# Zero products and reordered loads in the first stage, and another pacing of the gate sums and dots, in a two-layer diffusion backbone

## Chip, core and metric

One core of a Trainium2 chip runs the whole kernel in one launch. The metric is device microseconds of one execution. The kernel before took 2444.27 us (median of 3 runs, 2444.13 to 2444.34).

## What is computed

Two layers over 256 latent tokens (2048 wide, float32) and 256 context tokens. Each sub-layer is modulated by six vectors (shift, scale and gate for the mixer, and the same for the FFN) that come from a matrix product of SiLU(c) with `ada_w`.

```python
for i in range(DEPTH):                                  # 2 layers
    sh1, sc1, g1, sh2, sc2, g2 = split(silu(c) @ ada_w[i] + ada_b[i], 6)
    a = h * (1 + sc1) + sh1
    if i == 0:                                          # neighbourhood attention, context keys included
        csh1, csc1, ... = split(silu(c_ctx) @ ada_w[0] + ada_b[0], 6)
        ac = ctx * (1 + csc1) + csh1
        y = attention(a @ w_qkv, ac @ w_kv) @ w_o       # 16 heads of 128
    else:                                               # gMLP on chunks of 128 positions
        u, v = split(gelu(a @ w_in)); y = (u * (W_s @ ln(v) + b)) @ w_out
    h = layer_norm(ALPHA * h + g1 * y)
    h = layer_norm(ALPHA * h + g2 * swiglu(h * (1 + sc2) + sh2))   # FFN, inner width 5632
```

## The kernel before

Precision. Every large matrix product is done with three TensorE products: both operands are split into a rounded high part and a low part (`split_into`: ScalarE casts, VectorE subtracts), and high x high, high x low and low x high are summed in PSUM (`mm3`, lines 89 to 91). So every weight piece of 128 x 1024 costs ScalarE a cast, VectorE a subtraction whose two inputs lie in SBUF, and TensorE its products. `prefetch` keeps up to `pos["bufs"] - 1` pieces split ahead: two in the attention, four later.

First stage. Shift and scale of the mixer of layer 0 are needed for all 16 blocks (kt) of 128 columns before anything else. Block kt's scale is a TensorE dot (`dot`): 16 small float32 products with `c_pad` (SiLU(c) and SiLU(c_ctx), padded to 32 columns) in four column groups, then a copy to a row (ScalarE) and small products that gather the groups (`gather`, line 363). The shift is done so for kt < DVE0 = 3. From DVE0 on it is a VectorE dot (`dot_dve`): two passes over a 128 x 2048 tile of the transposed matrix, one for each condition. `modulate` then makes the block's activations on ScalarE and splits them. In the loop over kt TensorE does the keys of three heads, the dots of a block ahead (kt + 2 from kt = 2 on), the values of four token blocks, and from kt = 3 on an early piece of other keys. Loads go out from SP's queue in program order: `ap` (1 MB each, two a block, in four slots), `xt`, `rkv`. Small loads (`badj`, `ident`, `sel`) go out from ScalarE's queue, the rows of c and c_ctx from SP's, and GpSimd broadcasts them.

Tasks. The other modulation vectors are made in the background. A list of tasks stands in a fixed order: dots (VectorE, 1.2 us each, line 153) and gate products (VectorE multiplies and adds a 128 x 1024 piece into `gate`, line 177). After the 32 products of one gate vector a sum task runs an all-reduce over partitions on GpSimd (line 192). Each task costs 0.5 credits. Every step of the main loops calls `tick(n)`, which adds n x rate credits and runs the tasks that they pay for; `pace(units)` sets the rate to all open credits over a number of units. A tick that has a side task (an affine step or a transposition of the FFN) counts 0.3. In the attention a piece of keys or values counts 2 units and half a query projection 1, 124 in all. An FFN has 172 ticks in its gate and up blocks (two blocks of 512 columns in turn, eight weight pieces each, the first with four), and its down-projection 78 more. `need(...)` runs what is left of a vector where it is used. Gate products and dots are pinned in VectorE's order; otherwise a scheduler orders each engine's instructions by priority. GpSimd has only sums, broadcasts of rows and memsets.

Accumulators. Four PSUM tiles (`acc`) serve the gate and the up product of a block in turn; the down-projection needs all four at once, so it waits until VectorE has multiplied `sg` (line 820).

Of the kernel before, what the change touches and what calls it, by code (L numbers as in the profile page):

```python
# [11 lines left out]
F32 = mybir.dt.float32  # L12
F32R = mybir.dt.float32r
BF16 = mybir.dt.bfloat16
AF = mybir.ActivationFunctionType
ALU = mybir.AluOpType
# [3 lines left out]
P = 128  # L20
D = 2048
NT = 256
KT = D // P
# [12 lines left out]
MASKED = -1e30  # L36

SH1, SC1, G1, SH2, SC2, G2 = range(6)
HK0 = 3
RAW = 4  # L40
ADA = 6
FETCH = 5
SCRATCH = 4096
BUSY = 0.3
DVE0 = 3
W0 = HK0 * P + 512
EARLY = tuple((3 + 4 * g + h, h, 4 * g) for g in range(3) for h in range(4))
EN = 4
EARLY_END = {HK0 + h: 12 for h in range(4)}


@with_exitstack
def hybrid_kernel(ctx: ExitStack, tc: tile.TileContext, i, out):
    nc = tc.nc
    V, S, T = nc.vector, nc.scalar, nc.tensor
# [1 line left out]
    outer = ctx.enter_context(tc.tile_pool(name="outer", bufs=1))  # L57

    c_col = outer.tile([P, KT, 2], F32, tag="ccol", name="c_col")
    nc.sync.dma_start(c_col, i["c_col"])  # L60
    badj = outer.tile([P, 2, 6, KT], F32, tag="badj", name="badj")
    nc.scalar.dma_start(badj, i["ada_b_col"])
    ident = outer.tile([P, P], F32, tag="ident", name="ident")
    nc.scalar.dma_start(ident, i["ident"])
    eps_t = outer.tile([P, 1], F32, tag="eps", name="eps_t")
    nc.gpsimd.memset(eps_t, EPS)
    warm = outer.tile([P, 1], F32, tag="warm", name="warm")
    S.activation(c_col, c_col, AF.Silu)
    for t in (SC1, SC2):
        V.tensor_scalar(badj[:, :, t, :], badj[:, :, t, :], 1.0, None, ALU.add)  # L70
    lncol = outer.tile([P, 4, 2, KT], F32, tag="lncol", name="lncol")
    cols = outer.tile([P, 2, 6, KT], F32, tag="cols", name="cols")
    cols2 = outer.tile([P, 2, 6, KT], F32, tag="cols2", name="cols2")
# [7 lines left out]
    def spread(dst, src):  # L81
        nc.sync.dma_start(dst[0:1, :], src[None, :])
        nc.gpsimd.partition_broadcast(dst, dst[0:1, :])

    def pin(ins):
        return tc.keep_in_program_order(ins)
# [6 lines left out]
    def split_into(hi, lo, src):  # L93
        S.copy(hi, src)  # L94
        V.tensor_tensor(lo, src, hi.bitcast(F32), ALU.subtract)  # L95
# [93 lines left out]
    def sum_task(layer, t):  # L189
        def run():  # L190
            g = gate[(layer, t)]
            nc.gpsimd.partition_all_reduce(g, g, P, ReduceOp.add)
        return [(layer, t), 0.5, run, None]

    tasks, side = [], []
    state = {"credit": 0.0, "rate": 0.0}
# [36 lines left out]
    def pace(units):  # L233
        state["rate"] = sum(t[1] for t in tasks) / units
# [8 lines left out]
    for h in range(NH):  # L243
        if h in EARLY_END:
            enqueue(i["w_k"][h - HK0][:, EARLY_END[h] * P :], f"wk{h}", ((KT - EARLY_END[h]) * P,))
        elif h >= HK0:
            enqueue(i["w_k"][h - HK0], f"wk{h}")
        enqueue(i["w_q"][h], f"wq{h}")
# [29 lines left out]
    with tc.tile_pool(name="attnX", bufs=1) as px, ExitStack() as late:  # L278
# [21 lines left out]
        with tc.tile_pool(name="st", bufs=1) as st:  # L300
# [11 lines left out]
            def fetch(kt):  # L312
# [2 lines left out]
                    held[kt, t] = load_st(src, f"ap{kt}{t}", 2 * kt + t)  # L315
                load_x(kt)

            c_pad = st.tile([P, KT, 32], F32, tag="cpad", name="c_pad")
            nc.gpsimd.memset(c_pad, 0.0)
            V.tensor_copy(c_pad[:, :, 0:2], c_col)  # L320
            sel = st.tile([P, 2], F32, tag="sel", name="sel")
            nc.scalar.dma_start(sel, i["sel"])
            mod = st.tile([P, 2, KT, 2], F32, tag="mod", name="mod")
            kps = [stp_pool.tile([P, 512], F32, tag=f"k{h}", name=f"kps{h}") for h in range(HK0)]
            vps = [stp_pool.tile([P, 512], F32, tag=f"v{b}", name=f"vps{b}") for b in range(4)]
# [17 lines left out]
            def dot(kt, t):  # L343
                if t and kt >= DVE0:
                    return dot_dve(kt, t)
                if t == 0:
                    dps[kt] = stp_pool.tile([P, 512], F32, tag="a", name=f"aps{kt}")
                r = held.pop((kt, t))
                for kk in range(KT):
                    g = 32 * (kk % 4)  # L350
                    pin(T.matmul(
                        dps[kt][g : g + 32, t * P : (t + 1) * P], c_pad[:, kk, :], r[:, kk * P : (kk + 1) * P],
                        start=kk < 4, stop=kk >= KT - 4, tile_position=(0, g),
                    ))

            def gather(kt):
                ps = dps.pop(kt)
                ts = 1 if kt >= DVE0 else 2
                row = st.tile([P, 2 * P], F32, tag="row", name=f"row{kt}", bufs=1)
                S.copy(row[:, 0 : ts * P], ps[:, 0 : ts * P])  # L360
                o = ps[:, 256:260].rearrange("p (t b) -> p t b", t=2)
                for t in range(ts):
                    pin(T.matmul(o[:, t, :], row[:, t * P : (t + 1) * P], sel, start=True, stop=True))
                for t, ada in enumerate((SC1, SH1)[:ts]):
                    V.tensor_scalar(mod[:, t, kt, :], o[:, t, :], badj[:, 0, ada, kt : kt + 1], None, ALU.add)
# [5 lines left out]
            def modulate(kt):  # L371
                tmp = st.tile([P, 512], F32, tag="tmp", name=f"tmp{kt}", bufs=2)
                for b in range(2):
                    sl = slice(b * 256, (b + 1) * 256)
                    S.activation(
                        tmp[:, sl], xt[kt][:, sl], AF.Identity,
                        bias=mod[:, 1, kt, b : b + 1], scale=mod[:, 0, kt, b : b + 1],
                    )
                split_into(ah[:, kt, :], al[:, kt, :], tmp)

            for n, bc in enumerate((c_bc, cc_bc)):
                spread(bc, i["c_rows"][n])
            fetch(0)
            prefetch(1)
            fetch(1)
            for t in range(2):
                dot(0, t)
            gather(0)
            modulate(0)
            for kt in range(KT):  # L390
                hi, lo = piece()
                first, last = kt == 0, kt == KT - 1

                def keys(h):
                    c = slice(h * P, (h + 1) * P)
                    mm3(kps[h], hi[:, c], lo[:, c], ah[:, kt, :], al[:, kt, :], first, last, pin)

                def values(b):
                    c, tb = slice(HK0 * P, W0), slice(b * P, (b + 1) * P)
                    mm3(vps[b], ah[:, kt, tb], al[:, kt, tb], hi[:, c], lo[:, c], first, last, pin)  # L400

                def dots(k):
                    if k < KT:
                        if k > 2:
                            fetch(k)
                        for t in range(2):
                            dot(k, t)

                def rows(k):
                    if k < KT:  # L410
                        gather(k)

                ahead = kt + 2 if kt > 1 else kt + 1
                keys(0)
                if kt == 2:
                    rows(3)
                keys(1)
                keys(2)
                dots(ahead)
                values(0)  # L420
                values(1)
                rows(ahead)
                values(2)
                values(3)
                if kt == 0:
                    modulate(1)
                    for bc in (c_bc, cc_bc):
                        pin(S.activation(bc, bc, AF.Silu))
                    fetch(2)
                if kt == 1:  # L430
                    modulate(2)
                    dots(3)
                    pos["bufs"], pos["pin"] = 3, False
                for at, h, k0 in EARLY:
                    if at == kt:
                        h += HK0
                        hi, lo = piece()
                        ps = stp_pool.tile([P, 512], F32, tag="a", name=f"eps{h}{k0}")
                        for j in range(EN):
                            c = slice(j * P, (j + 1) * P)  # L440
                            mm3(ps, hi[:, c], lo[:, c], ah[:, k0 + j, :], al[:, k0 + j, :], j == 0, j == EN - 1, pin)
                        if h in early:
                            V.tensor_tensor(early[h], ps, early[h], ALU.add)
                        else:
                            free = NH - 2 * (h - HK0 + 1)
                            early[h] = oT[:, free : free + 2, :].rearrange("p a b -> p (a b)")
                            V.tensor_copy(early[h], ps)
                if 1 < kt and kt + 1 < KT:
                    modulate(kt + 1)
            nc.sync.dma_start(lncol, i["ln_col"])  # L450
        pa = late.enter_context(tc.tile_pool(name="attnA", bufs=1))
        for h in range(HK0):
            put_k(h, kps[h])
# [386 lines left out]
    affine_tasks(h_t, i["ln_row"][0], "a0")  # L840
    add_tasks(0, G2)
    add_tasks(1, SH1, SC1, SH2, SC2)
    pace(245)
    m2 = []

    def begin(b, st):
# [20 lines left out]
    st = stats_tile("v")  # L867
# [43 lines left out]
    )  # L911
    affine_tasks(h_t, i["ln_row"][2], "a2")
    add_tasks(1, G2)
    pace(170)
    lr = []

    def last_rows():
# [127 lines left out]
```

## Time and profile before

| | |
|---|---|
| profiled execution | 2446.65 us |
| its span | 2444.9 us |
| TensorE busy | 2381.0 us, 97% |
| weight loads (PEld) | 1977.7 us, 81% |
| VectorE busy | 1764.2 us, 72% |
| ScalarE busy | 1122.7 us, 46% |
| GpSimd busy | 109.7 us, 4% |
| HBM read | 606.46 MB, 249 GB/s over the span |

Busy times are sums over the span and overlap. TensorE is the engine that is nearly always busy, so what it waits for, and at which clock it runs, is what to look for. A granted clock of 1.00 is 2.4 GHz and 0.50 is 1.2 GHz. A product's duration is longer than its distance to the next one, because products are pipelined.

### The profile page before, as it was taken

To read this page: it belongs to the slowest core of one execution; us is meant where nothing else is said; L and a number is where in the kernel's file an instruction comes from. 1 tells how busy PE (TensorE), PEld (TensorE's weight loads), DVE (VectorE), ACT (ScalarE), POOL (GpSimd) and SP (SyncE) were. 2 spreads that over 40 slices of the span, in tenths; PEclk is the share of its full clock that TensorE was granted. 3 is DMA by queue.
4 is the path that set the end of the run, shared out by engine and by line. 5 is a ranking of instruction groups with operands and counts; after the bars stand their busy time and mean duration, and the time that the engine had idled before them with its cause. 6 is when DMAs were issued, how large, how long until landed. Compare 5 with 4: busy or idle time off the path is not lost. (4 is left out here: it accounts for less than half of the span.)

```text
span 2444.9 us, 31279 instructions
## 1 busy us (share of the span) xinstructions
PE 2381.0 (97%) x11574; PEld 1977.7 (81%) x11574; DVE 1764.2 (72%) x2158; ACT 1122.7 (46%) x1534; POOL 109.7 (4%) x54
## 2 busy tenths in 40 slices
PE   7999999998999999999999999999999999989998
PEld 5888988887788888888888788777888888878886
DVE  4877867577797877777888788787755555566666
ACT  3344534344644444444455554446444444435553
POOL 0000000001010100000000020020100000020000
PEclk9999999999999999999999999999999999999999
DMA  9977877765689899999989677746676766645563
GB/s 358 348 260 243 266 230 235 232 209 189 205 285 322 293 327 305 320 318 316 324 275 335 205 261 255 271 157 206 231 226 224 231 225 222 216 159 189 175 213 131
DMA packets 167680, 610.62 MB, mean 250 GB/s; under 512 B 19076, under 2 KB 21572, under 8 KB 163172
## 3 DMA queue, kind: packets, MB, share of 16 engines
q1 hardware_dynamic: 120888, 440.64, 54.1%
q10 hardware_dynamic: 46512, 167.96, 19.9%
q8 instruction: 90, 1.47, 0.2%
q14 instruction: 62, 0.51, 0.1%
q0 software_dynamic: 128, 0.03, 0.0%
HBM read 606.46 MB, written 2.10 MB: 249 GB/s over the span
## 5 line engine op out<-in xcount | busy, mean ns | idle before, releaser
L95 DVE TENSOR_TENSOR lwf<-rwf,hwf 128x1024 fp32r<-128x1024 f32 x320 | 401.7, 1257 | 288.3 <-ACT hwf L94 288.2
L94 ACT CAST hwf<-rwf 128x1024 fp32r<-128x1024 f32 x320 | 336.8, 1053 | 482.8 <-PE pu L91 236.1
L89 PE MATMUL pod<-hwd,ghd 128*128 128x512 f32 x684 | 267.6, 391 | 7.7 <-DVE sg L820 7.7
L95 DVE TENSOR_TENSOR lwd<-rwd,hwd 128x1024 fp32r<-128x1024 f32 x172 | 220.4, 1283 | 67.8 <-ACT hwd L94 67.8
L91 PE MATMUL pod<-hwd,gld 128*128 128x512 f32 x684 | 266.7, 391 | 1.1 <-DVE gld L95 1.1
L90 PE MATMUL pod<-lwd,ghd 128*128 128x512 f32 x684 | 267.2, 391 | 0.0
L153 DVE SCALAR_TENSOR_TENSOR ad<-ad,c_bc 128x1024 f32<-128x1024 f32 x192 | 232.6, 1218 | 0.9 <-DMA ad<-in_ada_t 0.9
L94 ACT CAST hwd<-rwd 128x1024 fp32r<-128x1024 f32 x172 | 180.2, 1048 | 53.3 <-PE pod L91 31.7
L177 DVE SCALAR_TENSOR_TENSOR gate<-ag,c_col,gate 128x1024 f32<-128x1024 f32 x128 | 163.2, 1281 | 0.1
L89 PEld LDWEIGHTS pod<-hwd,ghd 128*128 128x128 f32 x684 | 129.1, 189 | 35.4 <-DVE sg L820 8.4
L91 PEld LDWEIGHTS pod<-hwd,gld 128*128 128x128 f32 x684 | 128.9, 189 | 28.6 <-DVE gld L95 1.5
L90 PEld LDWEIGHTS pod<-lwd,ghd 128*128 128x128 f32 x684 | 129.0, 189 | 26.2
L89 PE MATMUL pg<-hwf,f0h 128*128 128x512 f32 x320 | 126.4, 395 | 0.0
L89 PE MATMUL pg<-hwf,f1h 128*128 128x512 f32 x320 | 126.4, 395 | 0.0
L90 PE MATMUL pu<-lwf,f0h 128*128 128x512 f32 x320 | 124.6, 389 | 0.1
L91 PE MATMUL pg<-hwf,f0l 128*128 128x512 f32 x320 | 124.7, 390 | 0.0
L91 PE MATMUL pg<-hwf,f1l 128*128 128x512 f32 x320 | 124.7, 390 | 0.0
L91 PE MATMUL pu<-hwf,f0l 128*128 128x512 f32 x320 | 124.5, 389 | 0.0
L89 PE MATMUL pu<-hwf,f0h 128*128 128x512 f32 x320 | 124.5, 389 | 0.0
L89 PE MATMUL pu<-hwf,f1h 128*128 128x512 f32 x320 | 124.5, 389 | 0.0
L90 PE MATMUL pu<-lwf,f1h 128*128 128x512 f32 x320 | 124.5, 389 | 0.0
L91 PE MATMUL pu<-hwf,f1l 128*128 128x512 f32 x320 | 124.5, 389 | 0.0
(338 smaller groups left out, 5332.9 us busy)
## 6 DMA issues: line engine op xcount, KB each, us to landing
rwf<-in_w_in_t SPq DMA_DIRECT2D x320, 512.0 KB
ad<-in_ada_t ACTq DMA_DIRECT2D x192, 512.0 KB
rwd<-in_w_out SPq DMA_DIRECT2D x176, 512.0 KB
ag<-in_ada_g ACTq DMA_DIRECT2D x128, 512.0 KB
rwg<-in_w_gin SPq DMA_DIRECT2D x64, 512.0 KB
ap<-in_ada_p SPq DMA_DIRECT2D x19, 1024.0 KB
rwq<-in_w_q SPq DMA_DIRECT2D x32, 512.0 KB
rwo<-in_w_o SPq DMA_DIRECT2D x32, 512.0 KB
```

Source lines behind the costliest of these rows:

```text
L89: keep(T.matmul(ps, sh, mh, start=first, stop=False))
L90: keep(T.matmul(ps, sh, ml, start=False, stop=False))
L91: keep(T.matmul(ps, sl, mh, start=False, stop=last))
L94: S.copy(hi, src)
L95: V.tensor_tensor(lo, src, hi.bitcast(F32), ALU.subtract)
L153: pin(V.scalar_tensor_tensor(r, r, 1.0, c_bc[:, half * 1024 : (half + 1) * 1024], ALU.mult, ALU.mult, accum_out=o[:, nt : nt + 1],))
L177: pin(V.scalar_tensor_tensor(g, loaded.pop(key), c_col[:, kt, 0:1], g, ALU.mult, ALU.add))
```

## The change

`DVE0` becomes 4, so block 3's shift is a TensorE dot too. A zero tile is filled by GpSimd, and `heat` issues products of it into a PSUM tile that is overwritten later: before the first dot, after each of the first two dots, and after the first gather. SiLU goes from ScalarE directly into `c_pad`; a dummy SiLU comes first. The small loads are reordered: the two rows of c go out from ScalarE's queue, only layer 0's half of `badj` is loaded at the start, `ident` and layer 1's half after the stage. Block 3 is modulated at kt = 2. The sum of layer 0's first gate costs 2.5 credits instead of 0.5; `pace(245)` becomes 235 in the first FFN and `pace(170)` becomes 160 in the second.

```diff
--- before.py
+++ after.py
@@ -36,13 +36,14 @@
 MASKED = -1e30
 
 SH1, SC1, G1, SH2, SC2, G2 = range(6)
+SUM_AT = {(0, G1): 2.5}
 HK0 = 3
 RAW = 4
 ADA = 6
 FETCH = 5
 SCRATCH = 4096
 BUSY = 0.3
-DVE0 = 3
+DVE0 = 4
 W0 = HK0 * P + 512
 EARLY = tuple((3 + 4 * g + h, h, 4 * g) for g in range(3) for h in range(4))
 EN = 4
@@ -57,17 +58,13 @@
     outer = ctx.enter_context(tc.tile_pool(name="outer", bufs=1))
 
     c_col = outer.tile([P, KT, 2], F32, tag="ccol", name="c_col")
-    nc.sync.dma_start(c_col, i["c_col"])
+    tc.keep_in_program_order(nc.sync.dma_start(c_col, i["c_col"]))
     badj = outer.tile([P, 2, 6, KT], F32, tag="badj", name="badj")
-    nc.scalar.dma_start(badj, i["ada_b_col"])
     ident = outer.tile([P, P], F32, tag="ident", name="ident")
-    nc.scalar.dma_start(ident, i["ident"])
     eps_t = outer.tile([P, 1], F32, tag="eps", name="eps_t")
     nc.gpsimd.memset(eps_t, EPS)
     warm = outer.tile([P, 1], F32, tag="warm", name="warm")
-    S.activation(c_col, c_col, AF.Silu)
-    for t in (SC1, SC2):
-        V.tensor_scalar(badj[:, :, t, :], badj[:, :, t, :], 1.0, None, ALU.add)
+    tc.keep_in_program_order(S.activation(warm, eps_t, AF.Silu))
     lncol = outer.tile([P, 4, 2, KT], F32, tag="lncol", name="lncol")
     cols = outer.tile([P, 2, 6, KT], F32, tag="cols", name="cols")
     cols2 = outer.tile([P, 2, 6, KT], F32, tag="cols2", name="cols2")
@@ -190,7 +187,7 @@
         def run():
             g = gate[(layer, t)]
             nc.gpsimd.partition_all_reduce(g, g, P, ReduceOp.add)
-        return [(layer, t), 0.5, run, None]
+        return [(layer, t), SUM_AT.get((layer, t), 0.5), run, None]
 
     tasks, side = [], []
     state = {"credit": 0.0, "rate": 0.0}
@@ -315,11 +312,15 @@
                     held[kt, t] = load_st(src, f"ap{kt}{t}", 2 * kt + t)
                 load_x(kt)
 
+            zero = st.tile([P, 512], F32, tag="zero", name="zero")
+            nc.gpsimd.memset(zero, 0.0)
             c_pad = st.tile([P, KT, 32], F32, tag="cpad", name="c_pad")
             nc.gpsimd.memset(c_pad, 0.0)
-            V.tensor_copy(c_pad[:, :, 0:2], c_col)
             sel = st.tile([P, 2], F32, tag="sel", name="sel")
-            nc.scalar.dma_start(sel, i["sel"])
+            pin(nc.scalar.dma_start(sel, i["sel"]))
+            pin(nc.scalar.dma_start(badj[:, 0], i["ada_b_col"][:, 0]))
+            pin(S.activation(c_pad[:, :, 0:2], c_col, AF.Silu))
+            pin(S.activation(c_col, c_col, AF.Silu))
             mod = st.tile([P, 2, KT, 2], F32, tag="mod", name="mod")
             kps = [stp_pool.tile([P, 512], F32, tag=f"k{h}", name=f"kps{h}") for h in range(HK0)]
             vps = [stp_pool.tile([P, 512], F32, tag=f"v{b}", name=f"vps{b}") for b in range(4)]
@@ -379,13 +380,25 @@
                 split_into(ah[:, kt, :], al[:, kt, :], tmp)
 
             for n, bc in enumerate((c_bc, cc_bc)):
-                spread(bc, i["c_rows"][n])
+                pin(nc.scalar.dma_start(bc[0:1, :], i["c_rows"][n][None, :]))
+                nc.gpsimd.partition_broadcast(bc, bc[0:1, :])
+            for t in (SC1, SC2):
+                V.tensor_scalar(badj[:, 0, t, :], badj[:, 0, t, :], 1.0, None, ALU.add)
+
+            def heat(n, width):
+                for _ in range(n):
+                    pin(T.matmul(vps[3][:, :width], zero[:, :P], zero[:, :width], start=True, stop=True))
+
+            heat(2, 512)
+            heat(1, 256)
             fetch(0)
             prefetch(1)
             fetch(1)
             for t in range(2):
                 dot(0, t)
+                heat(1, 256 - 128 * t)
             gather(0)
+            heat(3, 256)
             modulate(0)
             for kt in range(KT):
                 hi, lo = piece()
@@ -414,6 +427,7 @@
                 keys(0)
                 if kt == 2:
                     rows(3)
+                    modulate(3)
                 keys(1)
                 keys(2)
                 dots(ahead)
@@ -445,9 +459,13 @@
                             free = NH - 2 * (h - HK0 + 1)
                             early[h] = oT[:, free : free + 2, :].rearrange("p a b -> p (a b)")
                             V.tensor_copy(early[h], ps)
-                if 1 < kt and kt + 1 < KT:
+                if 2 < kt and kt + 1 < KT:
                     modulate(kt + 1)
             nc.sync.dma_start(lncol, i["ln_col"])
+            nc.sync.dma_start(ident, i["ident"])
+            nc.sync.dma_start(badj[:, 1], i["ada_b_col"][:, 1])
+            for t in (SC1, SC2):
+                V.tensor_scalar(badj[:, 1, t, :], badj[:, 1, t, :], 1.0, None, ALU.add)
         pa = late.enter_context(tc.tile_pool(name="attnA", bufs=1))
         for h in range(HK0):
             put_k(h, kps[h])
@@ -840,7 +858,7 @@
     affine_tasks(h_t, i["ln_row"][0], "a0")
     add_tasks(0, G2)
     add_tasks(1, SH1, SC1, SH2, SC2)
-    pace(245)
+    pace(235)
     m2 = []
 
     def begin(b, st):
@@ -911,7 +929,7 @@
     )
     affine_tasks(h_t, i["ln_row"][2], "a2")
     add_tasks(1, G2)
-    pace(170)
+    pace(160)
     lr = []
 
     def last_rows():
```

## Rows read from the trace of the kernel before

**Rows 1.** Stretches of 20 us: busy us (records) by engine, granted clock, DMA share, GB/s

```profile
20.00:40.00 20.00, 18.90 (x249) 14.42 (x249) 7.35 (x12) 11.09 (x15) 0.00 (x0) 1.00 1.02 409
...
80.00:100.00 20.00, 20.00 (x145) 16.02 (x145) 16.89 (x23) 6.91 (x12) 0.00 (x0) 1.00 0.98 351
...
640.00:660.00 20.00, 16.79 (x80) 12.76 (x79) 17.64 (x31) 12.69 (x25) 2.60 (x2) 1.00 0.46 147
...
820.00:840.00 20.00, 19.88 (x88) 16.12 (x87) 19.70 (x13) 7.38 (x7) 11.88 (x1) 1.00 0.68 231
...
1340.00:1360.00 20.00, 20.00 (x90) 16.57 (x89) 17.75 (x27) 9.51 (x14) 0.00 (x0) 1.00 0.83 271
...
1380.00:1400.00 20.00, 14.85 (x63) 11.38 (x61) 18.25 (x35) 11.17 (x20) 2.84 (x2) 0.83 0.52 182
```

**Rows 2.** What TensorE waited for, whole span: us in total, times, longest

```profile
PE pod L89 <- DVE sg L820: 7.7, 1, 7.7
...
PE pt L557 <- ACT p L547: 6.7, 1, 6.7
...
PE aps L363 <- ACT row L360: 4.3, 2, 3.8
...
PE ztm L670 <- DVE h_t L628: 3.0, 1, 3.0
```

**Rows 3.** Timeline of the first stage: start, us, engine, line, tile; idle before it

```profile
1.18 0.31 SPq L82 DMA_DIRECT2D c_bc<-in_c_rows  x1
...
1.81 0.83 SPq L307 DMA_DIRECT2D ap<-in_ada_p  x2
...
7.68 1.94 PE L351 MATMUL aps<-ap,c_pad 128*32 128x128 f32 x32 [7.68 <-DMA ap<-in_ada_p]
...
15.82 0.80 PE L89 MATMUL kps<-ah,hkv 128*128 128x512 f32 x1 [2.27 <-ACT ah L94]
...
38.08 1.08 PE L351 MATMUL aps<-ap,c_pad 128*32 128x128 f32 x32
...
39.15 2.29 DVE L338 SCALAR_TENSOR_TENSOR ap<-ap,c_bc 128x2048 f32<-128x2048 f32 x1
...
44.59 0.59 PE L363 MATMUL aps<-sel,row 128*128 128x2 f32 x2 [3.84 <-ACT row L360]
```

**Rows 4.** Stretches from restart to the clock's rise: TensorE busy, clock, DMA share, GB/s

```profile
44.59:50.26 5.67, 5.67 (x14) 0.50 1.01 368
...
561.30:565.68 4.38, 4.38 (x15) 0.50 0.98 337
...
1393.52:1398.26 4.74, 4.64 (x10) 0.50 0.54 164
...
2191.13:2197.24 6.11, 6.11 (x16) 0.50 0.53 174
```

**Rows 5.** Timeline at the end of attention: VectorE, TensorE, GpSimd

```profile
528.98 2.47 DVE L177 SCALAR_TENSOR_TENSOR gate<-ag,c_col,gate 128x1024 f32<-128x1024 f32 x2
...
534.47 1.22 DVE L95 TENSOR_TENSOR lwq<-rwq,hwq 128x1024 fp32r<-128x1024 f32 x1
...
542.92 1.04 PE L557 MATMUL pt<-ident,p 128*128 128x128 f32 x8
...
550.76 11.88 POOL L192 PARTITION_ALL_REDUCE gate<-gate  x1 [398.97 <-DVE gate L177]
...
552.43 7.99 DVE L95 TENSOR_TENSOR vl<-v,vh 128x512 fp32r<-128x512 f32 x1
```

**Rows 6.** Timeline of VectorE at the end of the first FFN

```profile
1384.07 1.21 DVE L153 SCALAR_TENSOR_TENSOR ad<-ad,c_bc 128x1024 f32<-128x1024 f32 x1
...
1386.34 0.26 DVE L614 BATCH_NORM_AGGREGATE mvm<-std 128x2 f32<-128x24 f32 x1
```

**Rows 7.** Timeline of VectorE during the last gate sum

```profile
2180.47 10.00 DVE L95 TENSOR_TENSOR lwd<-rwd,hwd 128x1024 fp32r<-128x1024 f32 x1 [0.30 <-ACT hwd L94]
```

**Rows 8.** Chain that ended last, 1560 to 1570 us: start, us, what

```profile
1562.59 0.87 PE sp L886 x4
```

## The prediction

> **What bounds the kernel now.** I read the table of windows first, 20 us each over the whole span, for the places where TensorE is not full. It is 97% busy, so only its 64 idle microseconds and its time at half clock can be earned. Four stretches matter for this change: the first 50 us, the end of attention, the end of the first FFN (5.15 us idle of 20, clock 0.83) and the end of the last FFN's blocks. A window like 820 to 840 loses only 0.12 us although a gate sum runs in it [rows 1]. The waits of TensorE then give the names: 7.7 us for VectorE's product `sg`, 6.7 us for the softmax weights `p`, 4.3 us for ScalarE's copy `row` (two waits, 3.8 the longer), 3.0 us for `h_t` [rows 2].
>
> The timelines tell the mechanisms. In the first stage loads run at 409 GB/s from 20 to 40 us [rows 1]; the first product starts at 7.68 us when `ap` has landed, and the keys of block 0 follow after a gap of 2.27 us. Block 3's shift is two VectorE passes of 2.29 us; ScalarE's queue stands behind their result, so the small copy that TensorE wants comes late: 3.84 us idle before 44.59 [rows 3]. After each of the four stalls TensorE restarts at a granted clock of 0.50, its 1.2 GHz level, for 5.67, 4.38, 4.74 and 6.11 us of work, each costing about half its length: 2.8, 2.2, 2.3 (4.64 busy) and 3.1 us [rows 4]. The clock column says 1.00 before 20 us, but a 512-column product there takes 0.80 us and a block of 32 small ones 1.94 us [rows 3], so I take that start as half speed too.
>
> A gate sum is an all-reduce on GpSimd of 11.88 us that starts 0.1 us after the last gate product, since GpSimd has nothing else. While it runs, VectorE's next splits stand: 7.99 us for one that reads two SBUF tiles [rows 5], 10.00 for another [rows 7]; about 9 us from the sum's start is waiting. The first sum meets head 15's softmax, the last one the product `sg` that frees the accumulators of the down-projection. At the end of the first FFN the last two dots run on VectorE from 1384.07, and only at 1386.34 does the aggregation `mvm` start, on which the next stage waits [rows 6].
>
> **The change, part by part.**
>
> *First stage, block 3.* The stall goes: 3.84 idle and 2.8 of half clock [rows 3, 4], 6.6 us. Added on TensorE: 32 small products, half of 1.94 us at full clock, 1.0 with the gather. Net gain 5.6. Next late is block 4's VectorE dot; it has as cover a block's 33 products of 0.227 us (90 recorded in 20.00 us [rows 1], a few records missing) and a dot, 8.5 us, for 4.6 us of work, but if block 3's split fell behind it in VectorE's queue some 2.5 us would come back (an estimate: the dot from about 37.3 to 42, the split wanted near 40).
>
> *First stage, head.* The two row loads leave SP's queue, so `ap` goes out at 1.18 instead of 1.81: 0.63 us [rows 3]. The zero products: two of 512 and one of 256 columns. Four records of 256 columns, two such products, take 0.87 us at full clock [rows 8], so these cost 2.2 us, or 4.3 at half clock, from about 1.4 us (after the memset) to 5.7, before `ap` can land at 7.0; they delay nothing. The later ones fall into the wait for the second transfer and into the 2.27 us gap; the last three (1.3 us; 2.6 if the clock is still low) just fit. If the clock is up at the dots, the second dot saves 0.97, the gather 0.5 and seven of the nine key products half of 0.40 each (5.67 us for 14 [rows 4]), 1.4: with the 0.63 that is 3.5. If it isn't raised: 0.6 minus 0.3 for the last zero products. I take 2.4, nearer the first, since TensorE has no long gap left there. Silu straight into `c_pad`, the pinned small loads, the later `ident` and `badj`: ScalarE and SP are idle or waiting beside them, nothing, at most 0.3 either way. The loads cap this: up to block 4's first dot they are 12.6 MB (nine `ap` of 1.05, four `xt` and one early piece of 0.26, four `rkv` of 0.46); the first has landed at 7.05, the other 11.5 at 409 GB/s by 35.2. TensorE came for it at 38.08 [rows 3] and will at 35.6, with 3.5 gained and 1.0 added. So 8.0 for the stage, 3.4 (head not raised, block 3's split late) to 9.1.
>
> *First gate sum.* A credit of 2.5 at an unchanged 126 units raises the rate from 0.385 to 0.401 per unit. The sum itself is popped at unit 126 as before, but the 32nd gate product moves from unit 125 to unit 120. That is the place of the pair at 528.98, ending 531.45 [rows 5]. So the sum runs from about 531.6, and the first split it stops is `lwq` at 534.47: until 540.6, done at 541.8. Behind it stands head 14's softmax: maximum, exp, reciprocal and scale twice, to 545.8 by the durations of such a chain. TensorE wants its transposes at 542.92 [rows 5]: 2.9 us idle; the 3.2 us lost in 640 to 660 left the clock at 1.00 [rows 1], so I count no half clock. Removed: 6.7 idle and 2.2 of half clock. Net 5.9; bounds 0 (as bad as before) and 8.9 (the order leaves it covered).
>
> The Trainium skill speaks against these moves. Page "SBUF — State Buffer", section "Who interferes with whom": a VectorE instruction with two SBUF inputs and a GpSimd instruction that reads SBUF contend, and the one that starts first holds the port pair for its whole length. The row agrees that it blocks, but the split that stood from 552.43 was done at 560.42, 2.2 us before the 11.88 us from 550.76 were over [rows 5]. By that rule the time would be that of the last rival below, about 2420 us.
>
> *Last gate sum.* Rate 16.5/160 instead of 16.5/170: the 32nd product falls on tick 161 instead of 171 of 172 (eight side tasks count 0.3 each). A tick is 12 products of 0.227 us, 2.72 us, so it moves 27 us earlier, into the gate half of the last block. There four split pieces are ready, about 10 us of work against 9 to 10 us of blocking; at 820 to 840 that cost 0.12 us [rows 1]. I take 0.3. Gain: 7.7 and 3.1, less 0.3: 10.5 (8.8 if the stretch costs 2).
>
> *Second gate sum and the dots of layer 1.* The sum moves from tick 55 to 53, within the same block: 0, plus or minus 0.4. The dots end at unit 235 instead of 245, and the loop has 243, so none is left at the end. `mvm` can start 2.3 us earlier [rows 6]. What is then late is the chain itself, as after the attention: 3.2 us idle at full clock in 640 to 660, against 5.15 here and 2.3 of half clock [rows 1, 4]. Gain 4.2; bounds 0 and 4.6.
>
> Sum: 8.0 + 5.9 + 10.5 + 4.2 = 28.6 us. Profiled execution: 2446.65 us, span 2444.9 and 1.75 around it; to 2418.0. It stands 2.4 above the median 2444.27, so the forecast for the median is 2415.7.
>
> **Rivals.**
> - *The first sum gives nothing.* Head 14's softmax stalls as head 15's did, or the sum waits for its later place in the queue. For it: my 2.9 us of idle is not far from the 3.84 us at which the clock fell [rows 3, 4]. Against: between the stopped split and the transposes stand most of a key projection and half a query projection. 2415.7 + 5.9 = 2421.6.
> - *Loads set the pace of the first stage.* From 80 to 100 us they ran at 351 GB/s with a DMA share of 0.98 [rows 1]. At that rate block 4's first load lands at 39.8, 4.2 us after TensorE wants it, and so much of the gain goes: 2419.9. Against: 409 GB/s from 20 to 40, with the same backlog.
> - *VectorE becomes the bound in the first FFN, the other side.* In its down-projection (78 ticks) VectorE is busy 17.75 of 20 us [rows 1], 2.41 of 2.72 per tick. The faster pace adds 0.028 dots of 1.3 us, 0.04 per tick. Beyond 2.72 each tick is longer by the excess: at 0.37 the 28.6 us are gone, from 0.43 it is slower by over 4.9 us, at 0.5 the time is 2415.7 + 78 x 0.5 = 2455. Against: 0.31 us of room against 0.04.
> - *VectorE stands for a sum's whole 11.88 us.* Then the transposes wait 2.9 us longer, and the last gate block's stretch costs 2.0 instead of 0.3: 2420.3. Against: 560.42 in [rows 5].
>
> **How the numbers follow.** Forecast 0.56, first sum 0.17, loads 0.14, whole length of the sum 0.04; VectorE as the bound 0.09, of which 0.05 end within 0.2% (4.9 us, about what a measurement of this kernel can tell from no change) and 0.04 slower. Predicted: 2415.7, the likeliest. Low end: 2444.27 less 9.1, 8.9, 10.8 and 4.6 is 2411; with 2 us for shifts in the order elsewhere, 2409. High end: the small ends of all parts (3.4, 0, 8.8, 0) give 2432; two rivals together give 2426. Range 2409 to 2432. Faster 0.91, same 0.05, slower 0.04.
>
> **What would show it.** Block 3's stall: no idle of 3.8 us near 40 us, kt = 4's keys about 8 us earlier. Head: the nine products of block 0 at 0.39 us instead of 0.63. First sum: an all-reduce some 20 us earlier against the end of attention, TensorE idle under 3 us at `pt`. Last sum: inside the last gate block, no wait of `pod` for `sg`. Dots: `mvm` right after its statistics, no half clock after 1380. The prediction is wrong if a sum stays at its old place, or if the full windows of the FFN show TensorE idle.

## The result, and the profile after

The changed kernel takes 2416.86 us (median of 4 runs, 2414.66 to 2419.84), the kernel before took 2444.20 in the same comparison (4 runs, 2443.64 to 2444.34): a ratio of 0.9889, 95% interval 0.9872 to 0.9906, or 27.3 us less. Forecast: 2415.7, range 2409 to 2432. The profiled execution took 2419.84 us with a span of 2418.1; TensorE is 98% busy in it.

The table of windows of the changed kernel; columns as in [rows 1] (busy us of PE, PEld, DVE, ACT, POOL, granted clock, DMA share, GB/s):

```profile
20.00:40.00 20.00, 18.98 (x272) 14.78 (x262) 6.72 (x13) 13.13 (x19) 0.00 (x0) 1.00 1.02 408
...
540.00:560.00 20.00, 16.79 (x90) 14.56 (x91) 14.42 (x26) 15.69 (x28) 1.12 (x1) 0.91 0.61 202
...
640.00:660.00 20.00, 16.79 (x73) 12.36 (x72) 14.15 (x24) 17.41 (x34) 2.60 (x2) 0.91 0.37 110
...
1380.00:1400.00 20.00, 17.45 (x86) 13.03 (x85) 15.75 (x26) 17.74 (x36) 2.59 (x2) 1.00 0.49 157
...
2140.00:2160.00 20.00, 20.00 (x90) 16.57 (x89) 16.09 (x9) 8.77 (x10) 8.83 (x1) 1.00 0.53 170
```

```profile
2136.95 11.88 POOL L189 PARTITION_ALL_REDUCE gate<-gate  x1 [413.50 <-DVE gate L174]
```

The end of the first FFN (1380 to 1400) lost 2.55 us at full clock where it lost 5.15 at 0.83 [rows 1]. The last gate sum now runs from 2136.95 to 2148.83, in the last gate block, and TensorE is full from 2100 to 2180. At 640 to 660 the idle time is what it was, 3.21 us, but the clock is 0.91 instead of 1.00.

What TensorE waited for in the changed kernel (us in total, times, longest), to hold against [rows 2]:

```profile
PE pt L575 <- ACT p L565: 3.7, 2, 3.4
...
PE aps L352 <- DMA ap<-in_ada_p: 1.9, 1, 1.9
...
PE aps L364 <- ACT row L361: 1.1, 1, 1.1
...
PE ztm L688 <- DVE h_t L646: 0.2, 1, 0.2
```

The wait for `sg` is gone, that for `p` is 3.7 instead of 6.7, that for `row` 1.1 instead of 4.3, that for `h_t` 0.2 instead of 3.0. The timeline of the changed kernel shows what stands in their place, first in the first stage (start, us, engine, line, tile; idle time before it in brackets):

```profile
1.35 4.64 PE L390 MATMUL vps<-zero 128*128 128x512 f32 x6 [1.35 <-POOL zero L316]
7.92 1.93 PE L352 MATMUL aps<-ap,c_pad 128*32 128x128 f32 x32 [1.93 <-DMA ap<-in_ada_p]
...
10.93 1.94 PE L352 MATMUL aps<-ap,c_pad 128*32 128x128 f32 x32
...
16.66 0.91 PE L86 MATMUL kps<-ah,hkv 128*128 128x512 f32 x1
...
19.16 0.39 PE L88 MATMUL kps<-ah,lkv 128*128 128x512 f32 x1
...
40.90 0.28 PE L364 MATMUL aps<-sel,row 128*128 128x2 f32 x2
...
41.35 2.28 DVE L339 SCALAR_TENSOR_TENSOR junk<-ap,oT 128x2048 bf16<-128x2048 f32 x1
...
46.90 0.22 DVE L342 TENSOR_SCALAR mod<-raw_c,badj 128x2 f32<-128x2 f32 x1
47.16 1.09 ACT L376 ACTIVATE tmp<-xt,mod 128x256 f32<-128x256 f32 x2 [3.50 <-DVE mod L342]
...
48.16 0.24 ACT L361 COPY row<-aps 128x128 f32<-128x128 f32 x1
...
48.45 0.38 PE L364 MATMUL aps<-sel,row 128*128 128x2 f32 x2 [1.14 <-ACT row L361]
```

In this execution the zero products brought nothing: the dots still take 1.93 us and block 0's keys begin later than before (16.66, [rows 3]: 15.82). And block 3's stall has a small successor. Block 4's VectorE dot stands in VectorE's queue behind the result of that block's `gather` (40.90), so it starts only at 41.35. It ends at 46.0, ScalarE's queue stands 3.50 us on its result, and behind it waits block 5's `row`, which TensorE wants at 47.3. Around the first gate sum (GpSimd, VectorE, TensorE):

```profile
528.88 12.24 POOL L189 PARTITION_ALL_REDUCE gate<-gate  x1 [381.68 <-DVE gate L174]
...
530.59 8.84 DVE L92 TENSOR_TENSOR lwq<-rwq,hwq 128x1024 fp32r<-128x1024 f32 x1
...
542.58 0.33 PE L575 MATMUL pt<-ident,p 128*128 128x128 f32 x1 [3.37 <-ACT p L565]
```

The stopped split is `lwq`, as forecast, and head 14's softmax behind it is late: 3.37 us, and the clock falls behind it (0.91 in the window). The half clock lasts until 546.6 (TensorE's busy time, clock, DMA share, GB/s):

```profile
542.58:546.60 4.02, 3.74 (x17) 0.58 0.13 16
```

To compare stages I take marks from each trace: the starts of the first query product, of the last product of the output projection, and so on. Differences of marks leave out what happens elsewhere. In us, one execution each; runs of the section below stand under their labels:

| kernel | first stage (to first `qps`) | attention (to last `powo`) | first FFN (to first `gv`) | gMLP (to first `pogo`) | output (to first `pg`) | last FFN (to last `pod`) |
|---|---|---|---|---|---|---|
| before | 160.7 | 488.3 | 744.5 | 194.5 | 100.2 | 744.7 |
| changed | 156.2 | 486.2 | 741.6 | 189.0 | 98.3 | 735.0 |
| p_first | 153.5 | 488.8 | 747.2 | 191.0 | 97.3 | 745.9 |
| p_sumat | 159.8 | 486.6 | 745.5 | 192.2 | 100.0 | 744.7 |
| p_dots235 | 160.0 | 489.1 | 740.8 | 191.1 | 98.6 | 745.7 |
| p_last160 | 160.3 | 489.1 | 746.5 | 194.1 | 100.0 | 733.9 |
| after_again | 153.5 | 486.4 | 739.8 | 189.6 | 98.4 | 735.1 |
| a_noheat | 156.3 | 486.7 | 740.5 | 190.6 | 98.3 | 733.8 |
| a_heatmore | 153.7 | 486.5 | 739.8 | 187.3 | 98.3 | 733.9 |
| a_oldsum | 153.9 | 488.5 | 740.2 | 188.8 | 98.6 | 733.9 |
| a_olddots | 153.5 | 486.4 | 747.0 | 190.9 | 100.8 | 733.9 |
| a_oldlast | 153.9 | 486.4 | 740.9 | 190.1 | 98.4 | 744.3 |
| a_sumV | 153.3 | 479.2 | 742.2 | 190.9 | 98.4 | 733.9 |
| best | 154.0 | 479.2 | 740.4 | 194.0 | 98.1 | 733.8 |

First stage, first FFN and last FFN each fall into two groups, with the edit and without it (the first stage with a middle group of 156 where the first dots were slow), and the attention into three: 488.3 to 489.1 with the old place of the sum, 486.2 to 486.7 with the credit, 479.2 in `a_sumV` and `best`. The gMLP and the output projection behind it, which no edit touches directly, vary by 7 and 3.5 us.

### The profile page after: what moved, and what is told of

It reads as the page before. It is cut to its first block, busy times and chain, and to the rows that moved or that the text cites. A ratio compares the mean times of both kernels' runs of the same rounds, so it can differ in the third digit from the quotient of the medians.

```text
span 2418.1 us, 31362 instructions
## 1 busy us (share of the span) xinstructions
PE 2381.7 (98%) x11624; PEld 1977.0 (82%) x11624; DVE 1755.7 (73%) x2155; ACT 1122.7 (46%) x1536; POOL 109.8 (5%) x55
## 5 line engine op out<-in xcount | busy, mean ns | idle before, releaser
L92 DVE TENSOR_TENSOR lwf<-rwf,hwf 128x1024 fp32r<-128x1024 f32 x320 | 407.2, 1275 | 278.9 <-ACT hwf L91 278.6
L92 DVE TENSOR_TENSOR lwd<-rwd,hwd 128x1024 fp32r<-128x1024 f32 x172 | 212.2, 1235 | 64.0 <-ACT hwd L91 63.8
L87 PE MATMUL pg<-lwf,f0h 128*128 128x512 f32 x320 | 124.6, 389 | 0.4 <-DVE lwf L92 0.4
```

Of the source, the lines that this page charges most:

```text
L87: keep(T.matmul(ps, sh, ml, start=False, stop=False))
```

## Experiments

**The four parts alone, on the kernel before** (median of before here 2444.32, 23 runs from 2441.91 to 2449.92).

```diff
 p_last160
-    pace(170)
+    pace(160)
 p_dots235
-    pace(245)
+    pace(235)
 p_sumat
+SUM_AT = {(0, G1): 2.5}
-        return [(layer, t), 0.5, run, None]
+        return [(layer, t), SUM_AT.get((layer, t), 0.5), run, None]
 p_first
 (all other hunks of the change)
```

> The kernel before with the last pace alone, 170 to 160. Theory (the last gate sum costs TensorE 7.7 us at sg and 3.1 us of half clock, and costs 0.3 inside a steady gate block): about 10.5 us less than before, 2433.7, and no wait of pod for sg. Rival (VectorE stands for the sum's whole 11.88 us, so the stretch in the last block costs 2): 8.8 less. Rival (the last stage's gain in the whole change hangs on other parts, because they shift its phase): under 6 less.

Measured: 2435.56 us (5 runs, 2428.97 to 2437.63), ratio 0.9958 (0.9945 to 0.9972), 8.8 less. No wait of `pod` for `sg` is left in the last FFN, which takes 733.9 us instead of 744.7. The stage gave its 10.8; the median shows less, with runs 8.7 us apart.

> The kernel before with the pace of layer 1's dots alone, 245 to 235. Theory (what goes is the idle time and the half clock at the end of the first FFN): 4.2 us less, 2440.0, and the gMLP stage keeps its wait of 4.2 us at sp. Rival (the dots also delayed the gMLP stage behind them, and its 4 us that came beside in the whole change are theirs): 8 us less, and the wait at sp is about 2 us.

Measured: 2440.81 us (11 runs), ratio 0.9985 (0.9976 to 0.9993), 3.5 less (by the interval 1.7 to 5.9, which holds the prediction's 4.2). The first FFN gains 3.7 by the marks against before and 4.7 to 6.4 against the other kernels with the old pace. The wait at `sp` is 2.6 us instead of 4.2, but in p_sumat, with the old pace, it is 2.5 as well: the rival that gave the gMLP's 4 us to the dots is not borne out.

> The kernel before with the credit of the first gate sum alone, 0.5 to 2.5. Theory from the trace after (the stall moves from head 15's softmax to head 14's: 3.4 us idle and some 1.4 of half clock stand where 6.7 and 2.2 stood): about 4 us less, 2440. Prediction's term: 5.9 less, 2438.3. Rival (nothing is gained): 2444.

Measured: 2444.92 us (11 runs), ratio 1.0004 (0.9995 to 1.0013): the rival by the median, although the stall shrank as the theory says. TensorE's wait in p_sumat:

```profile
PE pt L558 <- ACT p L548: 3.7, 2, 3.4
```

The attention takes 486.6 us instead of 488.3 to 489.1. So by the marks about 2 us are there; the interval of the whole leaves room for 1.2 less at most. The faster rate also costs something: with it the split `lwq` comes late at a query projection early in the attention, a wait of 0.5 us that every kernel with this credit has and none without it.

> The kernel before with all edits of the first stage (zero products, reordered small loads, block 3's shift on TensorE), the paces and the sum's credit as before. Theory from the trace after: 5 us less, 2439.2, of which 0.5 in the head and 4.5 at block 3 (a stall of 1.1 us at the fifth block takes part of it back). Prediction's term: 8.0 less, 2436.2. Rival (loads set the pace of the stage and give it back before the end of the stage): under 4 less.

Measured: 2437.47 us (7 runs, 2432.43 to 2444.55), ratio 0.9973 (0.9961 to 0.9984), 6.9 less, nearer to the prediction's 8.0 than to the 5 that I had read from the changed kernel's trace, with both inside the interval (3.9 to 9.5). The same code behaved otherwise here: the first dots took 1.15 and 1.08 us, block 0's keys began at 13.71, and the stage ended at 153.5 instead of 156.2.

**The changed kernel again, and its zero products** (before here 2445.5, 7 runs from 2441.8 to 2448.23).

> The changed kernel once more, beside the three variants of it below. Theory (the parts add up in place: by the marks in the traces the first stage gives 4 to 7 us, the first sum 2.4, the dots about 5 and 2 to 3 more in the gMLP, the last sum 10.5; the four parts alone, measured one by one, gave 6.9, nothing, 3.5 and 8.8, 18.6 in all, because each median carries 2 to 3 us of clock falls elsewhere): 2417, with runs between 2412 and 2421. Rival (the parts really give 18.6, and the first four runs were lucky): 2423 or more.

Measured: 2416.98 us (4 runs, 2416.34 to 2418.46), ratio 0.9886 (0.9869 to 0.9902). The first four runs were no luck. The head in this execution:

```profile
1.35 4.63 PE L390 MATMUL vps<-zero 128*128 128x512 f32 x6 [1.35 <-POOL zero L316]
6.27 1.58 PE L352 MATMUL aps<-ap,c_pad 128*32 128x128 f32 x32 [0.28 <-DMA ap<-in_ada_p]
...
9.17 1.08 PE L352 MATMUL aps<-ap,c_pad 128*32 128x128 f32 x32 [0.69 <-DMA ap<-in_ada_p]
...
13.62 0.49 PE L86 MATMUL kps<-ah,hkv 128*128 128x512 f32 x1 [0.88 <-ACT ah L91]
```

The first load landed 1.65 us earlier than in the first profile, TensorE was idle 0.28 us instead of 1.93, the clock rose within the first dot, and the keys begin 3.04 us earlier.

```diff
 a_noheat: the zero tile, heat() and its calls removed
 a_heatmore
-            heat(1, 256)
+            heat(3, 256)
             fetch(0)
```

> The changed kernel without the zero products; the reordered small loads stay. Theory (the zero products raise the clock for the first dots only in executions where the first load lands soon after them, so they are worth 0 to 3 us): dots of 1.94 us, block 0's keys at about 15.2 us, and 1 to 2 us more than the changed kernel. Rival (they only stand in the way of the second dot and are worth nothing): the same time or 0.5 less.

Measured: 2419.74 us (4 runs, 2419.49 to 2420.71), 2.8 more than after_again, and the two sets of runs don't overlap; the first stage takes 156.3 us instead of 153.5. Here the zero products are worth 2.8 us, more than I expected, and the rival is out. In an execution with slow dots they are worth nothing: the one of 2419.84 us, profiled first, had a first stage of 156.2. The head without them has its first load at 6.62, so the earlier issue stays, and the products shown at half speed:

```profile
6.62 1.94 PE L350 MATMUL aps<-ap,c_pad 128*32 128x128 f32 x32 [6.62 <-DMA ap<-in_ada_p]
9.30 1.93 PE L350 MATMUL aps<-ap,c_pad 128*32 128x128 f32 x32 [0.75 <-DMA ap<-in_ada_p]
11.73 1.01 PE L362 MATMUL aps<-sel,row 128*128 128x2 f32 x4 [0.49 <-ACT row L359]
15.02 0.80 PE L86 MATMUL kps<-ah,hkv 128*128 128x512 f32 x1 [2.28 <-ACT ah L91]
```

> The changed kernel with two more zero products of 256 columns ahead of the first dot, so that TensorE isn't idle for the 1.9 us in which the profiled execution of the changed kernel waited for its first load. Theory (that idle time lost the clock): both first dots at about 1.1 us, block 0's keys before 14.6 us, 1 to 3 us less than the changed kernel. Rival (the clock rises by chance of its phase, whatever stands in that gap): in this execution too the dots may take 1.94, and the median is that of the changed kernel or 0.5 more.

Measured: 2416.19 us (4 runs, 2413.04 to 2417.18), 0.8 less than after_again, with overlapping runs. The head as the theory has it, without a gap ahead of the first dot:

```profile
1.35 5.84 PE L390 MATMUL vps<-zero 128*128 128x512 f32 x10 [1.35 <-POOL zero L316]
7.12 1.08 PE L352 MATMUL aps<-ap,c_pad 128*32 128x128 f32 x32
...
13.75 0.50 PE L86 MATMUL kps<-ah,hkv 128*128 128x512 f32 x1 [0.88 <-ACT ah L91]
```

But after_again was as fast there. Of the nine profiled executions with zero products only the first had slow dots throughout, the one with the gap of 1.93 us ahead of the first dot; in the other eight that gap was 0 to 1.06. That the gap is the cause is likely, and not shown.

**The first sum in another place.** The gate's 32 products come after ten dots instead of after all 64.

```diff
 a_sumV
-SUM_AT = {(0, G1): 2.5}
+SUM_AT = {}
+NDOT = 10
         add_tasks(0, SH2, SC2, G1)
+        tasks[:] = tasks[:NDOT] + tasks[64:] + tasks[NDOT:64]
```

> The changed kernel with the gate products of the attention's gate put behind ten dots instead of behind all 64, so that the first sum falls at the end of the second value projection, where no softmax is due; the credit of the sum is the old 0.5. Theory (the first sum's stall is only moved by the changed credit; in a stretch where the next split is wanted 3 us after VectorE is free again it costs nothing): no wait for p beyond 0.5 us, the attention (from its first query projection to the end of the output projection) 481 us instead of 486, 4 to 6 us less than the changed kernel. Rival (a stopped VectorE makes the next key projection late there): a wait for lwk of 2 to 5 us, and the same time.

Measured: 2410.43 us (4 runs, 2407.41 to 2411.55), ratio 0.9855 (0.9841 to 0.9870), 6.6 less than after_again, and the attention takes 479.2 us instead of 486.4. GpSimd, VectorE and the first product of the next key projection:

```profile
324.51 11.88 POOL L190 PARTITION_ALL_REDUCE gate<-gate  x1 [180.19 <-DVE gate L175]
...
327.11 7.59 DVE L93 TENSOR_TENSOR lwk<-rwk,hwk 128x1024 fp32r<-128x1024 f32 x1 [2.71 <-ACT hwk L92]
...
338.17 0.39 PE L87 MATMUL kps<-ah,hwk 128*128 128x512 f32 x1
```

The split takes 6.4 us longer than its 1.2 and is done at 334.70, ahead of the projection's first product; the next split runs at 335.77. There is no wait for `p` and none for `lwk`, and TensorE is full in that window (the columns as above):

```profile
320.00:340.00 20.00, 20.00 (x98) 16.85 (x97) 15.78 (x12) 6.25 (x11) 11.88 (x1) 1.00 0.52 169
```

At this place the sum costs TensorE nothing, because what it stops is not wanted soon. Held against it, the sum costs 9.1 us in the kernel before (488.3 to 479.2) and 7.0 in the changed one.

**Single edits taken back from the changed kernel** (before here 2443.17, 9 runs from 2438.78 to 2447.18). They are held against after_again, which ran on another chip, where before stood at 2445.5. These 2.3 us can be the spread of its runs; if they are the chip's, each difference below is 2.3 larger. The marks of these three kernels among themselves don't raise the question.

```diff
 a_oldsum
-SUM_AT = {(0, G1): 2.5}
+SUM_AT = {}
 a_olddots
-    pace(235)
+    pace(245)
 a_oldlast
-    pace(160)
+    pace(170)
```

> The changed kernel with the first sum's old credit, 0.5. Theory from the marks in the traces (with the changed credit the attention takes 486.3 us from its first query projection to the end of the output projection, with the old one 488.8): 2.5 us more than the changed kernel. Prediction's term: 5.9 more. Rival (the part alone gave nothing on the kernel before, so it gives nothing here): the same.

Measured: 2417.97 us (4 runs, 2415.90 to 2418.74), 1.0 more than after_again, with overlapping runs; the attention takes 488.5 us instead of 486.4 (486.4 in the next two kernels as well). The first sum's new credit is worth 1 to 2 us, 3.3 at most by the other reckoning.

> The changed kernel with the dots' old pace, 245. Theory (the parts add up in place; the traces show about 5 us up to the start of the gMLP and 2 to 3 more in it): 7 us more than the changed kernel, with TensorE idle about 5 us between 1260 and 1400 more than there. Prediction's term: 4.2 more. Rival (what the part alone gave on the kernel before): 3.5 more.

Measured: 2425.15 us (5 runs, 2422.02 to 2426.04), 8.2 more. The first FFN takes 747.0 us instead of 739.8 (740.2 and 740.9 in the other two). These three stalls of TensorE stand there, 7.2 us in all, one of them in the middle of the down-projection, where after_again loses 2.5 us from 1360 to 1400 and nothing from 1260 to 1300; half clock follows the last:

```profile
1274.65 0.74 PE L88 MATMUL pod<-hwd,gld 128*128 128x512 f32 x2 [1.41 <-DVE gld L92]
...
1383.40 1.25 PE L688 MATMUL ztm<-ident,h_t 128*128 128x128 f32 x8 [3.47 <-DVE h_t L646]
...
1386.95 0.80 PE L86 MATMUL gv<-hwg,m1h 128*128 128x512 f32 x1 [2.29 <-ACT m1h L91]
```

A fourth wait stands ahead of the first down-projection. In before, p_sumat and p_first, with the same old pace, there is none, and in p_last160 it is 0.3 us, so part of the 8.2 us may be this execution's own:

```profile
PE pod L86 <- DVE sg L838: 1.1, 1, 1.1
```

> The changed kernel with the last pace as before, 170. Theory (7.7 us idle at sg and 3.1 of half clock come back, the last FFN takes 745 us instead of 735): 10.5 more than the changed kernel. Rival (what the part alone gave on the kernel before): 8.8 more. If the whole is more than its parts because stalls that fall later in the run cost less where others are gone, the three together with the zero products and block 3 come to less than 27.

Measured: 2427.50 us (5 runs, 2426.73 to 2430.50), 10.5 more; `pod` waits 7.7 us for `sg` again, and the last FFN takes 744.3 us (733.9 in the two kernels above). As the theory has it.

**Both findings together**: a_heatmore's and a_sumV's edits.

> Two findings together: two more zero products of 256 columns ahead of the first dot, and the gate products of the attention behind ten dots, so that the first sum falls at the end of the second value projection. Theory (they don't touch each other): 0.8 and 6.5 less than the changed kernel, 2409.6, and no run above 2412. Rival (only the place of the sum counts): 2410.4, and runs as far apart as with it alone.

Measured: 2409.17 us (4 runs, 2407.79 to 2413.11), ratio 0.9858 (0.9843 to 0.9873). Faster than before by 34 us, and than the changed kernel by 7.8 (5.5 if each is held against before on its own chip); it can't be told from a_sumV, so the place of the sum is what counts. "No run above 2412" was missed: the profiled run was the one of 2413.11, with a wait of 4.5 us at `sp` in the gMLP and clock falls after it.

## Why the prediction was right, and where it was not

The time was right to 1.2 us and the sum to 1.3 (28.6 forecast, 27.3 measured). That closeness is partly luck: by the edits taken back, in runs and in marks, the first sum's term was some 4 to 5 us too large and the dots' term 3 to 4 too small. By the parts alone all four terms were too large, 28.6 against 18.6.

- **Last gate sum, 10.5: right.** 10.5 by taking it back, 10.8 by the marks, 8.8 alone by the runs. The sum ran in the last gate block, and the windows from 2100 to 2180 are full, so the 0.3 set aside for the stretch was not spent.
- **First gate sum, 5.9: mis-sized, 1.0 by the runs and 2.1 by the marks.** The stopped split and the late softmax were as forecast, and the sum moved by 17.3 us against the start of the attention (19.2 forecast). The step that failed is "2.9 us idle [...], so I count no half clock": the idle time is 3.4 us, followed by a second wait of 0.3, and the clock fell until 546.6, which costs 1.6 us more (an estimate: 3.74 us busy at 0.58). The faster rate adds waits of 0.5 for `lwq` and 0.35 for `qh`, which the prediction had at nothing. Together some 6 us stay where 2.9 were forecast. (By its own figures, 6.7 and 2.2 less 2.9, the term is 6.0 and not 5.9.) The argument was that a loss of 3.2 us at 640 to 660 had left the clock at 1.00 [rows 1]. But that loss was no single stall: it is made of several waits, the longest 1.62 us. And in the first profile of the changed kernel a loss of the same size did not leave the clock there. The rival "the first sum gives nothing" was nearer. Its time, 2421.6, wasn't met because the next term made up for it.
- **Dots of layer 1, 4.2: too small in the changed kernel, 8.2 by taking it back (7.2 by the marks); about right alone, 3.5 (3.7 to 6.4 by the marks).** What is left at the end is 2.5 us, not the 3.2 that I took from the end of the attention. And I looked only at the end, which is the step that failed: the wait of `pod` for `gld` in the middle of the down-projection goes too. In the kernel before it is

```profile
PE pod L91 <- DVE gld L95: 1.1, 1, 1.1
```

  and it stands in all five profiled kernels with the old pace (0.5 to 1.9 us) and in none of the nine with the faster one. Why the faster pace spares this wait, and not the opposite, the traces don't say.
- **First stage, 8.0: about right, 6.9 alone, 7.6 as what is left of 27.3 after 1.0, 8.2 and 10.5.** Head 2.4: the zero products alone are worth 2.8 by the runs. That I set it between 0.3 and 3.5 for two cases was right: executions show both. Block 0's last key product ended at 20.03 before, at 19.55 in the first profile of the changed kernel and at 16.46 in after_again, 0.5 and 3.6 earlier (the lines of before and of after_again):

```profile
19.64 0.39 PE L91 MATMUL kps<-ah,lkv 128*128 128x512 f32 x1
...
16.07 0.39 PE L88 MATMUL kps<-ah,lkv 128*128 128x512 f32 x1
```

  Block 3, 5.6: too large. With the earlier issue it is 3.9 by the marks (160.2, the mean of four kernels without the edits, to 156.3 in a_noheat). The step that failed is the cover of "block 4's VectorE dot", 8.5 us for 4.6 of work. The dot starts at 41.35, behind that block's `gather`, and not near the 37.3 that I estimated; and I counted until TensorE needs block 4, and not until ScalarE, stopped on that dot, has to copy block 5's row. It is the mechanism of the stall removed, one block later, at 1.1 us instead of 3.8 and without half clock. The keys at kt = 4 began 5.0 us earlier than before in the first profile and 7.7 in after_again, where about 8 were forecast. That wait is not the whole of the difference; the rest stays open.
- **The rivals of the loads and of VectorE as the bound** did not occur: 408 GB/s from 20 to 40 us, and full windows from 1140 to 1360. But where the head gained, the loads begin to show, about where the prediction put their cap (TensorE at 35.6): in after_again two dots wait 0.43 and 0.44 us for `ap`, the first of them block 4's.

```profile
35.76 1.08 PE L352 MATMUL aps<-ap,c_pad 128*32 128x128 f32 x32 [0.43 <-DMA ap<-in_ada_p]
```

- **VectorE standing the whole 11.88 us** didn't either: `lwq` was done at 539.43, 1.7 us before the sum's end at 541.12, `lwk` in a_sumV at 334.70, 1.7 before 336.39; before it was 2.2 [rows 5]. The Trainium skill ("SBUF — State Buffer", "Who interferes with whom") has the second of two such instructions blocked while the first holds the ports; these rows agree that it blocks, and show it released before the end of the all-reduce as it is recorded. The profile's spans of GpSimd are rough, so the 1.7 to 2.2 us are too.

One thing stays open. The parts alone sum to 18.6 us (6.9, 3.5, 8.8, and a loss of 0.6 for the first sum), the whole gives 27.3. The intervals of the four are 2 to 3 us wide to each side, so much of the gap can be their noise: each median carries clock falls in stages that the edit doesn't touch. All of it they hardly are: taken as independent, the four make some 5 us and the whole 4 (estimates from the intervals), together less than the gap of 8.7. The marks of the four parts, 6.7, 1.7 to 2.5, 3.7 to 6.4 and 10.8, make 23 to 26. Taken back from the changed kernel, the edits give 1.0, 8.2, 10.5 and 2.8, with 3.9 for block 3 by the marks 26.4 of 27.3. That is too near to the 27 which a_oldlast's expectation set as the bound to decide between parts that add up and stalls that cost less where others are gone, and with 2.3 us more for each of the three edits it would be 33. So the stalls that each edit removes are shown, and that their prices add up is likely, but not shown.

## What to carry to other kernels

Where an instruction stops another engine's queue for some 9 us, look for a place where what is queued next isn't wanted for that long, and move it there; shifting it by a few steps here only moved the stall to the softmax of the head before. A stall that is removed can be succeeded by the same wait one step later, so follow every queue that stood behind it, and not only the engine that shows it. Judge an edit in the stage that it touches, by marks in the trace: here identical code differs by 1 to 12 us from run to run.

## What the runs showed of the hardware

The length of a stall does not alone decide the granted clock after it. A wait of 1.31 to 1.62 us for `f0h` after the attention stands in every trace. It is 1.62 in the first profile of the changed kernel and in after_again, the same kernel; in the first, products of 0.63 us follow it and the window's clock is 0.91 (above), in the second the clock is 1.00 (two lines of the first, one of the second):

```profile
644.44 0.49 PE L86 MATMUL pg<-hwt,f0h 128*128 128x512 f32 x1 [1.62 <-ACT f0h L91]
...
646.15 0.63 PE L87 MATMUL pg<-lwt,f0h 128*128 128x512 f32 x1
...
640.00:660.00 20.00, 16.72 (x79) 12.56 (x78) 13.73 (x23) 16.73 (x35) 2.59 (x2) 1.00 0.53 176
```

A start behaves alike. The same six records of zero products took 4.60 to 4.64 us in six executions and 3.90 in a_sumV's. By these durations the clock had risen there before they ended, and had fallen again at the last three zero products (2.91 us there, 1.54 in after_again). The Trainium skill ("TensorE: Matmul & The Clock Gate", Part 1) says that the number of slow products at a kernel's start varies from run to run; these executions agree.
